# A gated delta-rule chain traced in closed stretches on VectorE, with the interleaved work tied behind them

## The chip, the core and the metric

The kernel runs on one core of one Trainium2 chip. The metric is the device time of one execution in microseconds (us), the median of several runs. TensorE (PE) multiplies matrices, VectorE (DVE) and ScalarE (ACT) work on whole tiles, GpSimd (POOL) is a slower third engine for such work, and SyncE (SP) issues the transfers. Each engine takes its instructions in the order in which they were placed, so an instruction that has to wait holds up all that stand behind it on its engine.

## The reference, cut to what matters

Two transformer-like blocks on 256 tokens of width 1024. The first is a token mixer and a feed-forward part; the second is a gated delta rule with a multi-scale pooling branch beside it, then a layer that picks among 16,384 experts. The change touches the delta rule alone:

```python
q, k = _l2norm(q), _l2norm(k)                     # x * rsqrt(sum(x*x) + 1e-6), 4 heads of 128
g = jnp.cumsum(g, axis=-1)
decay = jnp.exp(jnp.where(causal, g[..., :, None] - g[..., None, :], -jnp.inf))
a_mat = jnp.where(strict, jnp.einsum("bhnid,bhnjd->bhnij", k_beta, k) * decay, 0.0)
t_mat = lax.linalg.triangular_solve(eye + a_mat, eye, left_side=True, lower=True)
w_vals = jnp.einsum("bhnij,bhnjd->bhnid", t_mat, v_beta)
...                                               # a scan over chunks with a state per head
pooled = running_mean(p, window) - p              # windows 2, 4, 8, 16, a matrix each behind it
x = x + jnp.concatenate([o, pool_out], axis=-1) @ w_out
```

## The kernel before

All weights come from HBM in tiles of 128x1024. Each is split into a high part (`whi`, on ScalarE, line 210) and a low part (`wlo`, mostly on VectorE, line 223), and each projection of 128 output columns is 24 matmuls of 256 columns: 8 blocks of the inner size times three products of high and low parts (lines 366 to 368). Their results go to one of three PSUM buffers `pb`, and VectorE evacuates them (`ct`, `pp` or `zt`, a product with the row norm `rbs`), which frees the buffer.

`delta` runs two generators against each other with `weave`. **The chain** (`main`): four convolutions of k (`head`), cumulative sums of the gate, the decay matrix `dec` and its strict part `N`, sums of squares of k, their inverse root `yk` by a bit shift and three Newton steps (`rsqrt_steps`), Gram products of k (`gk`, line 1527), the spread of `byk` (line 455), N from all of these (lines 1533 and 1536), and then the inverse of eight unit triangular matrices of 128x128 (two halves `tb` of the sequence times four heads). The inverse first builds the 16x16 diagonal blocks `dg` (lines 611 to 615), copies them over the partitions with selection products (line 622, copied out to `rep` on line 624), inverts them in 15 steps of a product and a reduction on VectorE (lines 629 and 632), puts the blocks into `Z`, and doubles the block size in three levels (products on line 1566, masks on line 1576, sums on line 1571). Value products, state and output follow. **The fillers** (`filler`): the 16 projections for q, v, pooling (p) and gate (z) with what follows them (convolution taps on line 1298, silu on line 1287, pooling windows on GpSimd on line 1416, pooling products on line 1460), and, when the chain is done, the pooling half of the output projection.

The order is made in two steps. At each `yield` of a number the chain lets fillers of that weight be traced, so a `yield` between two steps of the chain puts filler instructions between them. A scheduler then places all instructions, with those of the chain at a higher priority. In the kernel before, the Newton steps for `yk` run on GpSimd (`eng=G`, lines 431 to 439), there is a `yield` before each of them, and one after each of the 15 steps of the block inverse.

Of the kernel before, what the change touches and what calls it, by code (L numbers as in the profile page):

```python
# [16 lines left out]
ALU = mybir.AluOpType  # L17
# [147 lines left out]
TY = [1.20, 8.92]  # L165
YL = [0.2, 0.64, 1.60, 3.20, 0.64, 0.72, 0.48, 0.80, 0.40, 1.92, 1.20, 0.16]
LEAD2 = 3000
LEAD3 = 3000
# [15 lines left out]
MAIN = ""  # L184
# [78 lines left out]

def weave(tc, main, fill, engines="", lead=None, leads=None):
    debt = 0.0
    engines = {getattr(mybir.EngineType, e) for e in engines.split(",") if e}
    with ExitStack() as stack:
        if engines:
            stack.enter_context(tc.manual_schedule(engines=engines))
        while True:  # L270
            with tc.high_priority(LEAD if lead is None else leads[0] if leads else lead):
                w = next(main, None)
            if w is None:
                break
            debt += w
            while debt > 0:
                g = next(fill, None)
                if g is None:
                    debt = 0.0
                    break  # L280
                debt -= g
# [6 lines left out]
class Builder:  # L288
# [110 lines left out]

    def rsqrt_steps(self, src, n, mult, add=None, floor=None, out=None, pace=0.2, eng=None):  # L400
        nc, sm = self.nc, self.s1
        V = nc.vector
        v, y, t = (sm.tile([P, 16], F32, name=k, tag=k)[:, 0:n] for k in ("rv", "ry", "rt"))
        y = y if out is None else out
# [18 lines left out]
        if short:  # L423
            for c in (0.75, 0.1875, 3.0 / 1024):
                for sp, vp, yp, tp in cut:
                    V.scalar_tensor_tensor(tp, yp, vp, yp, ALU.mult, ALU.mult)
                for sp, vp, yp, tp in cut:
                    V.scalar_tensor_tensor(yp, tp, -c, yp, ALU.add, ALU.mult)
            return y
        if eng:  # L430
            v = v if mult else src
            for _ in range(3):
                yield pace
                eng.tensor_tensor(t, v, y, ALU.mult)
                eng.tensor_tensor(t, t, y, ALU.mult)
                eng.tensor_scalar(t, t, -0.5, 1.5, ALU.mult, ALU.add)
                eng.tensor_tensor(y, y, t, ALU.mult)
            return y
# [159 lines left out]
    def inverse16(self, pool, N, Z, nb, rep):  # L598
        nc = self.nc
        V, A = nc.vector, nc.scalar  # L600
        n = Z.shape[1]
# [6 lines left out]
        for a in range(nb):  # L608
# [3 lines left out]
            else:  # L612
                V.scalar_tensor_tensor(d, N[:, :, 16 * a:16 * a + 16], bm[:, a:a + 1], d if a else eye,
                                       ALU.mult, ALU.add)
        V.tensor_tensor(dg, dg, dg2, ALU.add)
        A.copy(zd, eye)
# [9 lines left out]
        for j in range(1, 16):  # L626
# [4 lines left out]
            for h in hv:  # L631
                V.tensor_reduce(zd[:, h, j:j + 1], tmp[:, h, 0:j + 1], mybir.AxisListType.X, ALU.add)
            yield 0.6
        for a in range(nb):
# [604 lines left out]
    def delta(self, xs, pre, rs):  # L1239
# [5 lines left out]
        with tc.tile_pool(name="del", bufs=1) as dp:  # L1245
# [239 lines left out]
            def sums(tb):  # L1485
# [3 lines left out]
                for h in range(4):  # L1489
                    mm(ss[:, h:h + 1], sq[:, h, :], self.ones[:, 0:1], start=True, stop=True)  # L1490
                V.scalar_tensor_tensor(so[:, tb * 4:tb * 4 + 4], ss[:, 0:4], 1.0 / P, qe[:, tb * 4:tb * 4 + 4],
                                       ALU.mult, ALU.add)

            def main():
                sl = [slice(0, 4), slice(4, 8)]
# [24 lines left out]
                yield YL[1]  # L1520
                yield from self.rsqrt_steps(ss[:, 0:8], 8, 1.0, 4e-6, out=yk, pace=YL[11], eng=G)
                V.tensor_tensor(byk, beta.rearrange("p b h -> p (b h)"), yk, ALU.mult)
                gk = [b4(self.pa()), b4(self.pa())]
                for tb in range(2):
                    ts = slice(tb * P, tb * P + P)
                    for h in range(4):
                        mm(gk[tb][:, h, :], k[:, h, ts], k[:, h, ts], start=True, stop=True)
                yield YL[1]
                for tb in range(2):
# [7 lines left out]
                    G.tensor_tensor(dec[:, sl[tb], :], dec[:, sl[tb], :], tri.unsqueeze(1).to_broadcast([P, 4, P]), ALU.mult)  # L1537
                next(inv)
                yield YL[2]
                next(inv)  # L1540
                yield YL[3]
                for w in inv:
                    yield YL[4]
# [97 lines left out]

            weave(tc, main(), fl, MAIN, LEAD3)
            st["acc"] = [self.pa() for _ in range(4)]
# [371 lines left out]
```

## Time and profile before

| | |
|---|---|
| median of 3 runs | 1428.66 us (1424.08 to 1431.24) |
| the profiled execution | 1422.52 us, of which its span is 1420.7 us |
| TensorE busy | 1347.7 us (95% of the span) |
| VectorE busy | 1002.0 us (71%) |
| ScalarE busy | 683.5 us (48%) |
| GpSimd busy | 284.3 us (20%) |
| mean granted TensorE clock | 0.978 of full speed |

Busy times overlap. The span is from the first to the last instruction; the time of the execution also holds what lies around it. The granted clock has two levels, 2.4 GHz (1.00) and 1.2 GHz (0.50); a window that shows a number between them holds a change. Matmuls are pipelined, so TensorE's busy time is not TensorE at its peak.

### The profile page before, as it was taken

The page shows a single profiled execution, that of the slowest core. Times are in us where ns is not written, and L with a number is a line of the kernel's source. Part 1 is how long each engine was busy: PE and PEld are TensorE (multiplying, and loading weights), DVE is VectorE, ACT ScalarE, POOL GpSimd, SP SyncE. Part 2 cuts the span into 40 slices and gives each one's busy share as a digit, 9 for nine tenths or more (in the row PEclk, how much of TensorE's full clock was granted, in tenths as well). Part 3 has the DMA queues.
Part 4 walks back from the last instruction along what each step waited for, and adds up shares of the span by engine and source line. Part 5 has one row for each costly group of instructions (what it writes and reads, how often), then busy time and mean ns, then how long its engine had stood idle before and what let it go on. Part 6 is the DMA issues. An engine that isn't in the chain of part 4 may idle for free.

```text
span 1420.7 us, 26854 instructions
## 1 busy us (share of the span) xinstructions
PE 1347.7 (95%) x10570; PEld 1256.6 (88%) x10570; DVE 1002.0 (71%) x2060; ACT 683.5 (48%) x1242; POOL 284.3 (20%) x244
## 2 busy tenths in 40 slices
PE   7989999999999879999879999999999999999998
PEld 6888989999989868999879999999998888888886
DVE  7865768888869955899974777777875555555554
ACT  3522455565566502564534554444444555555554
POOL 5511351100034400202341000000002222222221
PEclk9899999999999989999989999999999999999999
DMA  6231434665524402444445444444446666666663
GB/s 221 65 98 47 142 127 135 208 227 180 189 92 149 134 16 75 151 163 164 153 144 179 158 155 149 149 149 143 150 154 205 193 194 193 193 193 193 193 193 118
DMA packets 64318, 217.88 MB, mean 153 GB/s; under 512 B 10272, under 2 KB 11232, under 8 KB 64064
## 3 DMA queue, kind: packets, MB, share of 16 engines
q1 hardware_dynamic: 59376, 212.76, 45.9%
q0 software_dynamic: 976, 2.71, 0.7%
q8 instruction: 83, 1.36, 0.4%
q10 hardware_dynamic: 3840, 0.70, 0.4%
q14 instruction: 43, 0.35, 0.1%
HBM read 214.69 MB, written 1.44 MB: 152 GB/s over the span
## 4 chain that ended last, share of the span: by engine, by line
PE 70%; DVE 21%; issue 3%; ACT 3%; POOL 3%; DMA 1%; SPq 0%; ACTq 0%; DVEq 0%; POOLq 0%
PE pa L1923 24%; PE pb L366 10%; PE pb L368 9%; PE pb L367 9%; DVE wlo L223 5%; PE pa L367 3%; PE pa L366 3%; PE pa L368 3%; PE pa L1566 1%; DVE x L1866 1%; DVE scr L1687 1%; DVE eg L1870 1%; PE pb L1877 1%; ACT whi L210 1%; POOL wlo L223 1%
## 5 line engine op out<-in xcount | busy, mean ns | idle before, releaser
L210 ACT ACTIVATE whi<-raw 128x1024 fp32r<-128x1024 f32 x396 | 418.4, 1058 | 538.4 <-PE pb L367 248.5
L223 DVE TENSOR_TENSOR wlo<-raw,whi 128x1024 fp32r<-128x1024 f32 x368 | 457.5, 1244 | 252.7 <-ACT whi L210 251.0
L366 PE MATMUL pb<-xnh,whi 128*128 128x256 f32 x1024 | 297.2, 291 | 13.8 <-DVE scr L1851 8.3
L368 PE MATMUL pb<-xnh,wlo 128*128 128x256 f32 x1024 | 291.0, 285 | 11.5 <-POOL wlo L223 6.9
L367 PE MATMUL pb<-xnl,whi 128*128 128x256 f32 x1024 | 290.4, 284 | 0.0
L1923 PE MATMUL pa<-whi,up 128*128 128x512 f32 x1024 | 274.7, 389 | 0.0
L1923 PEld LDWEIGHTS pa<-whi,up 128*128 128x128 f32 x1024 | 192.1, 188 | 39.8
L366 PEld LDWEIGHTS pb<-xnh,whi 128*128 128x128 f32 x1024 | 196.9, 192 | 18.2 <-PE pb L368 12.9
L368 PEld LDWEIGHTS pb<-xnh,wlo 128*128 128x128 f32 x1024 | 196.8, 192 | 13.2 <-POOL wlo L223 7.3
L367 PEld LDWEIGHTS pb<-xnl,whi 128*128 128x128 f32 x1024 | 197.2, 193 | 0.0
L366 PE MATMUL pb<-xh,whi 128*128 128x256 f32 x648 | 187.3, 289 | 0.0
L367 PE MATMUL pb<-xl,whi 128*128 128x256 f32 x648 | 184.7, 285 | 0.1
L368 PE MATMUL pb<-xh,wlo 128*128 128x256 f32 x648 | 184.7, 285 | 0.0
L1923 PE MATMUL pa<-wlo,up 128*128 128x512 f32 x512 | 158.3, 389 | 0.0
L223 POOL TENSOR_TENSOR wlo<-raw,whi 128x1024 fp32r<-128x1024 f32 x33 | 92.0, 2791 | 181.4 <-ACT whi L210 171.4
L503 POOL TENSOR_TENSOR up<-hb,up 128x256 fp32r<-128x256 f32 x32 | 45.9, 1435 | 409.3 <-ACT up L502 409.3
L366 PEld LDWEIGHTS pb<-xh,whi 128*128 128x128 f32 x648 | 124.0, 191 | 0.9 <-ACT xh L568 0.2
L367 PEld LDWEIGHTS pb<-xl,whi 128*128 128x128 f32 x648 | 123.9, 191 | 0.8 <-DVE xl L569 0.3
L368 PEld LDWEIGHTS pb<-xh,wlo 128*128 128x128 f32 x648 | 123.6, 191 | 0.4
L1923 PEld LDWEIGHTS pa<-wlo,up 128*128 128x128 f32 x512 | 96.2, 188 | 19.9
L503 POOL TENSOR_TENSOR up<-scr,up 128x256 fp32r<-128x256 f32 x32 | 47.1, 1472 | 127.0 <-ACT up L502 127.0
L367 PE MATMUL pa<-al,whi 128*128 128x256 f32 x176 | 49.1, 281 | 0.0
(534 smaller groups left out, 2220.4 us busy)
## 6 DMA issues: line engine op xcount, KB each, us to landing
raw<-down SPq DMA_DIRECT2D x128, 512.0 KB, 3.3
raw<-up SPq DMA_DIRECT2D x128, 512.0 KB, 4.3
raw<-w_in SPq DMA_DIRECT2D x46, 512.0 KB, 3.3
raw<-w_up SPq DMA_DIRECT2D x44, 512.0 KB, 3.5
raw<-w_down SPq DMA_DIRECT2D x22, 512.0 KB, 3.7
raw<-w_out SPq DMA_DIRECT2D x16, 512.0 KB, 3.3
raw<-w_query SPq DMA_DIRECT2D x16, 512.0 KB, 3.4
x<-xT SPq DMA_DIRECT2D x4, 256.0 KB, 5.6
```

Of the source, the lines that this page charges most:

```text
L210: nc.scalar.activation(hi, self.raw[self.nh], AF.Copy)
L223: e.tensor_tensor(lo[:, a:z], raw[:, a:z], hi[:, a:z], ALU.subtract)
L366: mm(ps, w[0], x[0], start=start, stop=False, **k)
L367: mm(ps, w[0], x[1], start=False, stop=False, **k)
L368: mm(ps, w[1], x[0], start=False, stop=stop, **k)
L503: (eng or self.nc.vector).tensor_tensor(lo, src, hi.bitcast(F32), ALU.subtract)
L1566: mm(out[:, h], lh[:, tb * 4 + h, :], self.halves(rh[:, tb * 4 + h, :], l, odd), start=True, stop=True)
L1687: V.max_index(idx[:, 0:8], vals[:, 0:8], src)
L1866: V.tensor_tensor(e1, iota, over(self.i1t), ALU.is_equal)
L1870: V.tensor_tensor(eg[m], eg[0], over(self.gp[m]), ALU.mult)
L1877: mm(ps[:, n, :], e1[:, q, :, r], eg[m][:, q, :, r], start=(m == 0), stop=(m == 1))
L1923: mm(acc[tb * 2 + hf], a[:, ts], b[:, hf * 512:hf * 512 + 512], start=False, stop=(e == 127 and lo == 1), skip_group_check=True)
```

## The change

Four things are done. The Newton steps for `yk` go back to VectorE, in one run without a `yield` (`self.rsqrt`); the branch `eng` is removed. The `yield` between the Gram products and N goes, so that norm, N and diagonal blocks are traced without fillers between them; the weight of the `yield` in the convolutions (`YL[0]`) goes from 0.2 to 0.45. The 15 steps of the block inverse have one `yield` behind them all in place of one behind each. And `weave` is given a list `behind`: fillers that are traced once the list holds an instruction are placed behind it on that instruction's engine (VectorE), first behind the last instruction on the diagonal blocks, later behind the last reduction of the block inverse.

```diff
-YL = [0.2, 0.64, 1.60, 3.20, 0.64, 0.72, 0.48, 0.80, 0.40, 1.92, 1.20, 0.16]
+YL = [0.45, 0.64, 1.60, 3.20, 0.64, 0.72, 0.48, 0.80, 0.40, 1.92, 1.20, 0.16]
...
             while debt > 0:
-                g = next(fill, None)
+                with tc.issue_after(behind[0]) if behind else ExitStack():
+                    g = next(fill, None)
...
-        if eng:
-            v = v if mult else src
-            for _ in range(3):
-                yield pace
-                eng.tensor_tensor(t, v, y, ALU.mult)
-                eng.tensor_tensor(t, t, y, ALU.mult)
-                eng.tensor_scalar(t, t, -0.5, 1.5, ALU.mult, ALU.add)
-                eng.tensor_tensor(y, y, t, ALU.mult)
-            return y
...
-        V.tensor_tensor(dg, dg, dg2, ALU.add)
+        self.blocks = V.tensor_tensor(dg, dg, dg2, ALU.add).ins
...
             for h in hv:
-                V.tensor_reduce(zd[:, h, j:j + 1], tmp[:, h, 0:j + 1], mybir.AxisListType.X, ALU.add)
-            yield 0.6
+                last = V.tensor_reduce(zd[:, h, j:j + 1], tmp[:, h, 0:j + 1], mybir.AxisListType.X, ALU.add)
+        self.blocks = last.ins
+        yield 0.6
...
-                yield from self.rsqrt_steps(ss[:, 0:8], 8, 1.0, 4e-6, out=yk, pace=YL[11], eng=G)
+                self.rsqrt(ss[:, 0:8], 8, 1.0, 4e-6, out=yk)
...
                         mm(gk[tb][:, h, :], k[:, h, ts], k[:, h, ts], start=True, stop=True)
-                yield YL[1]
...
                 next(inv)
+                behind.append(self.blocks)
                 yield YL[2]
                 next(inv)
                 yield YL[3]
+                next(inv)
+                behind[0] = self.blocks
                 for w in inv:
                     yield YL[4]
...
-            weave(tc, main(), fl, MAIN, LEAD3)
+            weave(tc, main(), fl, MAIN, LEAD3, behind=behind)
```

What the scheduler makes of it is seen in the order of the instructions. Outside this stage the order is the same on every engine.

TensorE before, from the last projection matmul of the fillers to the first level of the inverse (`dg,sel` are the selection products, `con_base,Z` the transposes of Z, `xh,wlo` a projection):

```order
L368 MATMUL pb<-xh,wlo 128x256
L622 MATMUL pa<-dg,sel 128x128 x16
L1555 MATMUL pa<-con_base,Z 128x128 x8
L1566 MATMUL pa<-TT,N 128x64 x8
L1585 MATMUL pa<-q,k 128x128 x7
L1566 MATMUL pa<-Z,Y 128x64 x4
```

TensorE now, from the Gram products (`pa<-k`) to the first projection behind the selection products (`pc<-ones,sq` are column sums of squares, of k and then of q):

```order
L1522 MATMUL pa<-k 128x128 x8
L1362 MATMUL pc<-ones,sq 128x1 x12
L447 MATMUL pa<-con_base,byk 128x128 x8
L614 MATMUL pa<-dg,sel 128x128 x16
L1362 MATMUL pc<-ones,sq 128x1 x2
L367 MATMUL pb<-xh,whi 128x256
```

Before, all 16 filler projections stood ahead of the selection products and none behind them; now six full ones are done by then and ten stand behind, 72 matmuls ahead of the transposes of Z and the rest among the levels.

VectorE before, at the diagonal blocks `dg` (`wlo` is a weight split; `pw`, `z` and `zt` are pooling and gate fillers):

```order
L613 SCALAR_TENSOR_TENSOR dg<-N,con_del 128x128
L611 TENSOR_SCALAR dg_5775<-N,con_del 128x128
L223 TENSOR_TENSOR wlo<-raw,whi 128x1024
L1432 SCALAR_TENSOR_TENSOR pw<-pw,pp 128x256
L613 SCALAR_TENSOR_TENSOR dg<-N,con_del,dg 128x128
L1287 SCALAR_TENSOR_TENSOR z<-th,zt 128x256
```

VectorE now, from the end of the Newton steps to the diagonal blocks:

```order
L440 SCALAR_TENSOR_TENSOR yk<-rt,yk 128x4 x2
L1541 TENSOR_TENSOR kds<-kds,yk 128x4
L1517 TENSOR_TENSOR byk<-beta,yk 128x8
L1542 TENSOR_TENSOR beg<-beg,byk 128x4
L1543 TENSOR_SCALAR beg<-beg 128x4
L1527 SCALAR_TENSOR_TENSOR N<-pa,N 128x512
L1530 SCALAR_TENSOR_TENSOR N<-pa,yk,N 128x128 x4
L1527 SCALAR_TENSOR_TENSOR N<-pa,N 128x512
L1530 SCALAR_TENSOR_TENSOR N<-pa,yk,N 128x128 x4
L605 SCALAR_TENSOR_TENSOR dg<-N,con_del 128x128
```

No filler stands between the chain's instructions there any more; the first one is behind the last instruction on the blocks.

VectorE now, from the last reduction of the block inverse to VectorE's share of the writes of Z (`ct` evacuates a projection and frees its PSUM buffer; before, the writes of Z stood right behind the reduction):

```order
L624 TENSOR_REDUCE zd<-itmp 128x4 x2
L1291 SCALAR_TENSOR_TENSOR v<-ct,params,v 128x254
L223 TENSOR_TENSOR wlo<-raw,whi 128x1024
L1287 TENSOR_TENSOR ct<-pb,rbs 128x256
L223 TENSOR_TENSOR wlo<-raw,whi 128x1024
L631 TENSOR_SCALAR Z<-zd,con_del 128x8x16 x4
```

Two weight splits, a convolution tap and an evacuation have come between the inverse and Z.

## Rows read from the trace of the kernel before

**Rows 1.** The page's chain that ended last, shares of the span by engine.

```profile
PE 70%; DVE 21%; issue 3%; ACT 3%; POOL 3%; DMA 1%; SPq 0%; ACTq 0%; DVEq 0%; POOLq 0%
```

**Rows 2.** Waits of PE, 444 to 535 us: us in total, times, longest.

```profile
PE pa L1555 <- DVE Z L638: 8.8, 1, 8.8
PE pb L1460 <- POOL rt L435: 2.9, 1, 2.9
PE pb L1460 <- DVE pw L1432: 1.9, 1, 1.9
PE pa L1619 <- DVE vn L1615: 0.8, 1, 0.8
PE pc L1490 <- ACT osq L1488: 0.3, 1, 0.3
PE pa L1566 <- DVE rep L1576: 0.3, 1, 0.3
```

**Rows 3.** Windows of 1 us: busy PE, PEld, DVE, ACT, POOL; granted clock; DMA share, GB/s.

```profile
473.00:474.00 1.00, 0.18 (x1) 0.21 (x2) 1.00 (x4) 0.00 (x0) 1.00 (x2) 0.65 0.39 45
476.00:477.00 1.00, 1.00 (x8) 1.00 (x7) 0.78 (x3) 0.50 (x2) 0.84 (x4) 0.64 0.58 131
...
500.00:501.00 1.00, 0.00 (x0) 0.00 (x0) 1.00 (x9) 0.00 (x0) 0.00 (x0) 0.80 0.00 0
514.00:515.00 1.00, 1.00 (x11) 1.00 (x9) 0.93 (x4) 0.00 (x0) 0.00 (x0) 0.87 0.00 0
```

**Rows 4.** Timeline, PE: start, us, engine, line, operation, tiles, passes, idle before.

```profile
442.39 2.03 PE L1504 MATMUL pa<-con_del,gt 128*128 128x128 f32 x16
...
454.92 1.95 PE L1527 MATMUL pa<-k 128*128 128x128 f32 x16
...
457.42 1.84 PE L1369 MATMUL pc<-ones,sq 128*128 128x1 f32 x16
...
480.02 1.03 PE L455 MATMUL pa<-con_base,byk 128*128 128x128 f32 x8
...
494.29 3.73 PE L622 MATMUL pa<-dg,sel 128*128 128x128 f32 x32
506.78 1.94 PE L1555 MATMUL pa<-con_base,Z 128*128 128x128 f32 x8 [8.76 <-DVE Z L638]
...
525.28 1.90 PE L1566 MATMUL pa<-TT,N 128*128 128x64 f32 x16
```

**Rows 5.** Timeline of ACT: the squares of k.

```profile
453.90 1.38 ACT L517 ACTIVATE sq<-k 128x256 f32<-128x256 f32 x4
```

**Rows 6.** Timeline of DVE: small pairs, a split, taps, N, blocks, first and last inverse step.

```profile
425.04 0.22 DVE L419 TENSOR_SCALAR ry<-rv 128x1 int32<-128x1 int32 x2
...
460.27 1.21 DVE L223 TENSOR_TENSOR wlo<-raw,whi 128x1024 fp32r<-128x1024 f32 x1
...
461.80 0.86 DVE L1298 SCALAR_TENSOR_TENSOR v<-ct,params,v 128x255 f32<-128x255 f32 x2
...
482.20 1.28 DVE L1533 SCALAR_TENSOR_TENSOR N<-pa,N 128x512 f32<-128x512 f32 x2
...
485.46 0.41 DVE L1407 TENSOR_TENSOR zt<-pb,rbs 128x256 f32<-128x256 f32 x1
...
486.14 0.28 DVE L611 TENSOR_SCALAR dg<-N,con_del 128x128 f32<-128x128 f32 x1
...
496.94 0.25 DVE L629 TENSOR_TENSOR itmp<-zd,rep 128x8 f32<-128x8 f32 x2
...
504.30 0.34 DVE L632 TENSOR_REDUCE zd<-itmp 128x4 f32<-128x64 f32 x2
```

**Rows 7.** Timeline of POOL and DVE: two mask products, and VectorE beside one of them.

```profile
455.67 1.35 POOL L1537 TENSOR_TENSOR dec<-dec,con_del 128x512 f32<-128x512 f32 x1
...
465.46 1.46 POOL L1590 TENSOR_TENSOR egb<-egb,q 128x512 f32<-128x512 f32 x1 [8.45 <-DVE q L1287]
...
465.71 1.32 DVE L419 TENSOR_SCALAR yk<-rv 128x4 int32<-128x4 int32 x2
```

More of the change, by code (lines that the diff above doesn't have):

```diff
@@ L261, in drive, with weave @@
             return e.value
-def weave(tc, main, fill, engines="", lead=None, leads=None):
+def weave(tc, main, fill, engines="", lead=None, leads=None, behind=None):
     debt = 0.0
@@ L398, in rsqrt, with rsqrt_steps @@
         return drive(self.rsqrt_steps(*a, **k))
-    def rsqrt_steps(self, src, n, mult, add=None, floor=None, out=None, pace=0.2, eng=None):
+    def rsqrt_steps(self, src, n, mult, add=None, floor=None, out=None, pace=0.2):
         nc, sm = self.nc, self.s1
@@ L1492, in sums @@
                                        ALU.mult, ALU.add)
+            behind = []
             def main():
```

## The prediction

> **What bounds the kernel now.** I read the page's chain first: TensorE holds 70% of it and VectorE 21% [rows 1], so a change in one stage is worth what TensorE waits or runs slowly there. The change lies between 444 and 553 us, so I then read who TensorE waits for there. From 444 to 535 it waits 8.8 us for the diagonal blocks' inverse to reach Z, 2.9 and 1.9 us before the pooling products (the first on GpSimd, which the Newton steps share with the pooling windows, the second on VectorE), and 0.8 + 0.3 + 0.3 us at hand-offs of the chain: 15.0 us [rows 2]. Next the granted clock by microsecond. It falls from 2.4 to 1.2 GHz within the first and the last of the long idles (about 473.3 and 500.6) and is back at about 476.7 and 514.25 [rows 3]. Between the return of work (473.8 and 506.8) [rows 3, 4] and the return of the clock lie 2.9 and 7.45 us at half speed, so 1.4 + 3.7 = 5.1 us are lost. **Up for grabs: 20.1 us.** The matmuls themselves are the same before and after (297 projection matmuls between the cumulative sums and the end of the inverse, and the same chain products), so the forecast is 20.1 us less what comes back.
>
> **What the change does, with prices.** By the order listing, 57 projection matmuls instead of 89 stand ahead of the Gram products `gk`, and then none until the selection products have gone out; the other 240 follow, among the inverse's steps and its three doubling levels. So the old hole is filled and a new one is cut.
>
> *New hole: the closed stretch.* The Gram products start at 444.4 + 57 x 0.12 = 451.2 (89 projections took 10.5 us, 0.12 each) and take 1.95, to about 453.1 [rows 4]. The squares of k end at 455.3 [rows 5]; what stands ahead of them on ScalarE loses two convolution starts and gains a tanh and a copy, so I leave that time. The sums follow within 0.2 us. From 455.5 VectorE has the path to itself: 12 pairs of Newton instructions at 0.2 = 2.4 (a pair of such small ones reads 0.22), 0.2 for `byk`, half of the 1.03 us spread before the first decay product can start (0.5), 3.3 for the ten instructions on N (482.20 to 485.46), nine for the diagonal blocks at 0.28 = 2.5 [rows 4, 6], and some 0.4 us of hand-offs. That is 9.3 us, to 464.8. TensorE is in order and has nothing else queued: 464.8 - 453.1 = 11.7 us, of which 24 passes of column sums at 0.115 (2.8) and the spreads (1.0) [rows 4] are work. **Lost: 7.9 us.** Above that: the mask product of `dec` on GpSimd runs at 455.67 for 1.35 us, in the same microseconds as the Newton steps now. In the trace a pair of shift instructions took 1.32 us rather than 0.22 while a like GpSimd product ran [rows 6, 7]. So the bounds are 7.9 and 9.0; I take 8.5, since only part of the product lies beside the steps.
>
> The Trainium skill (SBUF — State Buffer, Who interferes with whom) states that a VectorE instruction with two SBUF inputs and a GpSimd instruction that reads SBUF exclude each other for a whole instruction. It speaks against putting the steps there, and by it the term is 9.0 and the time 1426.6; without any holding 7.9 and 1425.5. The 1.32 us row agrees in size.
>
> *Inverse.* After the blocks, VectorE runs: two silus, three splits of weights at 1.2, three evacuations and five convolution taps at 0.4, one small evacuation of 0.1, and the 15 inverse steps, 7.7 us (496.94 to 504.64) [rows 6]: 0.8 + 3.6 + 3.2 + 0.1 + 7.7 = 15.4, up to and with the third evacuation, which frees the PSUM buffer of the first pooling projection and which the order puts behind the last reduction. TensorE has until then the selection products (3.7), 8 passes of sums (0.9) and 48 projections (5.8) = 10.4 us [rows 4]. **Lost: 5.0 us** uncontended; GpSimd's `egb` product and its two clears now lie beside VectorE here, and one held pair costs 1.1 [rows 7], so 5.0 to 6.6; I take 5.6. The selection products start after an idle longer than both that dropped the clock [rows 3], so they run at 1.2 GHz; that cost, 1.4 to 3.7 us, lies inside this term, because VectorE and not TensorE decides when the wait ends.
>
> *Clock again.* That leaves TensorE idle for about 2 to 4 us before the pooling projection; both measured falls lie in idles of 2.9 us and more [rows 2, 3]. So 0 to 3.7 us; I take 1.4, the smaller measured loss.
>
> *Levels.* With 6 projections left among them, the doubling levels' VectorE results now stand in one queue with splits, taps and pooling. There are seven hand-offs from VectorE back to TensorE (Y, the level-0 sums, the two `rep` masks, the level-1 sums, the last Z, `vn`). Nearest row below: today's three hand-off waits, 1.4 us together [rows 2]; above, each waits for one split ahead of it, 7 x 1.2 = 8.4 [rows 6]. I take 1.4, because projections stand between product and use. *Tail:* 14 instead of 9 output-projection matmuls stand in front of the second half's value product: 5 x 0.12 = 0.6 us at most. Newton leaving GpSimd, the pacing constant and the removed branch cost nothing else; the 4.8 us of pooling waits [rows 2] are already in the 20.1.
>
> **How the numbers follow.** 8.5 + 5.6 + 1.4 + 1.4 + 0.6 = 17.5 us come back out of 20.1, a gain of 2.6. The profiled execution took 1422.52 (span 1420.7), 6.1 below the median of 1428.66; I set the difference against the median: **1426**. Bounds: 7.9 + 5.0 + 0 + 0 + 0 = 12.9 (gain 7.2, 1421.5), and 9.0 + 6.6 + 3.7 + 8.4 + 0.6 = 28.3 (loss 8.2, 1436.9). A measurement here can tell about 0.5%, 7.1 us, from no change.
>
> **Rivals.** *VectorE's backlog takes the place of the wait (slower).* Place: from the evacuation for the first pooling projection to the first level's Y. VectorE has there four splits (4.8), four Z writes (1.1, taking 0.28 each), four evacuations, ten taps, a silu and two pooling pieces (about 6.6): 12.5 us [rows 6]. TensorE has two projections and 20 more of their matmuls (8.2), the pooling product and the transposes (1.3), two groups of 16 passes (1.9 each) [rows 4]: 13.3. They are nearly level, so from about 1 us of holding on VectorE each further microsecond is TensorE's, at this and each later hand-off. At 8.4 instead of 1.4 the sum is 24.5 (1433.1); with the longer clock loss and all the holding behind the stretch (6.6) too, 27.8: 1436.4. For it: VectorE's queue is full here, and the trace shows it held by GpSimd. Against: seven in a row need a split just ahead each time. Chance 0.18 for slower by over 0.5%.
>
> *The fillers cover everything after the closed stretch (faster).* No second fall of the clock, no hand-off wait, no holding: 12.9 come back, 1421.5, and a little more if the sums and spreads keep the clock up. For it: the order puts projections between every product and its use. Chance 0.17 for faster by over 0.5%. That the change doesn't do what it says is out: the order shows the stretch closed. Within 0.5%: 0.65. The range 1419.5 to 1436.5 leaves out no more than 2 in 10 and reaches into both rivals.
>
> **What would show it.** Right: a TensorE wait for VectorE's N and diagonal blocks, near 455 to 465, of 8 to 9 us less the sums; no 8.8 us wait at the Z transposes; a wait of 2 to 4 us behind the inverse at a projection; granted clock 0.5 at the selection products, 1.00 at the levels. Wrong: the clock at 1.00 through the stretch, waits of over 1 us at most level products, or the second half's value product earlier or later than 535 us by over 7.

## The result, and the profile after

The changed kernel takes **1416.55 us** (median of 8, 1415.85 to 1419.46), the kernel before 1427.13 us beside it (median of 8, 1422.34 to 1431.24): ratio 0.9932, interval 0.9914 to 0.9951. It is faster than the range of the prediction allowed. Two later comparisons with more executions gave less: 1417.74 against 1423.13 (ratio 0.9970, 0.9953 to 0.9987) and 1418.61 against 1423.26 (0.9965, 0.9945 to 0.9985). Some executions of either kernel run 5 to 10 us longer at a mean granted clock of 0.968 to 0.974 (20 of 132 of the kernel before in the later comparisons, 3 of 24 of the changed one), and by their times (1428.66 and more) they were four of the eight of before in the first comparison, and none of the changed kernel's. The profiled executions are 1422.52 and 1416.37 us, spans 1420.7 and 1414.6: 6.1 us apart.

The waits of TensorE from 444 to 535 us, after (us in total, times, longest), to be set beside [rows 2]:

```profile
PE pa L614 <- DVE dg L607: 5.5, 1, 5.5
PE pb L367 <- DVE ct L1287: 3.5, 1, 3.5
PE pc L1362 <- ACT sq L509: 1.0, 1, 1.0
PE pa L447 <- DVE byk L1517: 0.5, 1, 0.5
PE pc L1362 <- DVE yk L420: 0.4, 1, 0.4
```

That is 10.9 us where there were 15.0. All that is left lies before 482 us; the doubling levels (485 to 521 us) have no wait in the list. TensorE's timeline (start, us, line, tiles, passes, idle before) shows the two holes and what ends them, beside [rows 4]:

```profile
450.69 1.95 PE L1522 MATMUL pa<-k 128*128 128x128 f32 x16
453.64 1.95 PE L1362 MATMUL pc<-ones,sq 128*128 128x1 f32 x16 [1.00 <-ACT sq L509]
456.00 1.84 PE L1362 MATMUL pc<-ones,sq 128*128 128x1 f32 x8 [0.41 <-DVE yk L420]
458.37 1.97 PE L447 MATMUL pa<-con_base,byk 128*128 128x128 f32 x8 [0.53 <-DVE byk L1517]
465.83 5.56 PE L614 MATMUL pa<-dg,sel 128*128 128x128 f32 x32 [5.50 <-DVE dg L607]
...
481.51 0.38 PE L367 MATMUL pb<-xh,whi 128*128 128x256 f32 x1 [3.48 <-DVE ct L1287]
...
484.49 1.03 PE L1552 MATMUL pa<-con_base,Z 128*128 128x128 f32 x8
```

The Z transposes, which waited 8.76 us in before, follow their projections at once. The spreads took 1.97 us instead of 1.03 and the selection products 5.56 instead of 3.73 [rows 4], because the clock was at its lower level. Windows of 1 us (columns as in [rows 3]):

```profile
455.00:456.00 1.00, 0.59 (x6) 0.53 (x6) 0.38 (x4) 0.20 (x1) 0.64 (x1) 0.93 0.00 0
456.00:457.00 1.00, 1.00 (x5) 1.00 (x6) 1.00 (x11) 0.00 (x0) 0.00 (x0) 0.50 0.00 0
...
469.00:470.00 1.00, 1.00 (x8) 1.00 (x8) 1.00 (x7) 0.88 (x2) 0.00 (x0) 0.75 0.89 348
...
480.00:481.00 1.00, 0.00 (x0) 0.00 (x0) 1.00 (x1) 0.91 (x4) 1.00 (x2) 1.00 0.03 8
```

It falls from 2.4 to 1.2 GHz at 455.9 us, among the column sums, and is back at 469.5. In the second hole, from 478.0 to 481.5, it stays at 1.00. VectorE's timeline shows the path that both holes follow: Newton steps, blocks, the last inverse step, the evacuation.

```profile
456.23 0.23 DVE L434 TENSOR_TENSOR rt<-rv,yk 128x4 f32<-128x4 f32 x2
...
457.80 0.23 DVE L440 SCALAR_TENSOR_TENSOR yk<-rt,yk 128x4 f32<-128x4 f32 x2
...
465.39 0.29 DVE L607 TENSOR_TENSOR dg<-dg,dg 128x128 f32<-128x128 f32 x1
...
479.25 0.34 DVE L624 TENSOR_REDUCE zd<-itmp 128x4 f32<-128x64 f32 x2
...
481.03 0.42 DVE L1287 TENSOR_TENSOR ct<-pb,rbs 128x256 f32<-128x256 f32 x1
```

GpSimd's last mask product of `dec` ended at 455.64 us, so nothing held the Newton steps:

```profile
454.37 1.27 POOL L1531 TENSOR_TENSOR dec<-dec,con_del 128x512 f32<-128x512 f32 x1
471.88 1.29 POOL L1587 TENSOR_TENSOR egb<-egb,q 128x512 f32<-128x512 f32 x1 [16.24 <-DVE zd L624]
```

The second half's values (`vb`) come near the end of the stage in both kernels. VectorE's timeline has them at 534.08 us in before,

```profile
534.08 1.12 DVE L1631 SCALAR_TENSOR_TENSOR vb<-pa,beg,vb 128x128 f32<-128x128 f32 x4 [1.25 <-PE pa L1629]
```

and at 528.24 after, so that 5.8 of the 6.1 us are won by there:

```profile
528.24 1.13 DVE L1628 SCALAR_TENSOR_TENSOR vb<-pa,beg,vb 128x128 f32<-128x128 f32 x4 [0.47 <-PE pa L1626]
```

Not all of this is the stage's own, since two executions do not reach the stage at the same time. The cumulative sums of the gate are the same instruction of TensorE in every run here. They begin at 442.39 us in before [rows 4] and at 442.01 after:

```profile
442.01 2.03 PE L1499 MATMUL pa<-con_del,gt 128*128 128x128 f32 x16
```

From there to `vb` it is 91.7 us in before and 86.2 after, so 5.5 us are the stage's and 0.4 was there ahead of it. Below, a stage is compared by this stretch.

### The profile page after: what moved, and what is told of

The parts are those of the page before. It is cut to its first block, busy times and chain, and to the rows that moved or that the text cites. A ratio compares the mean times of both kernels' runs of the same rounds, so it can differ in the third digit from the quotient of the medians.

```text
span 1414.6 us, 26852 instructions
## 1 busy us (share of the span) xinstructions
PE 1344.7 (95%) x10570; PEld 1255.3 (89%) x10570; DVE 1000.5 (71%) x2078; ACT 684.4 (48%) x1242; POOL 280.3 (20%) x232
## 3 DMA queue, kind: packets, MB, share of 16 engines
q0 software_dynamic: 976, 2.71, 0.7%
## 4 chain that ended last, share of the span: by engine, by line
PE 51%; DVE 14%; issue 2%; POOL 1%; ACT 1%; ACTq 0%; DVEq 0%
PE pa L1920 24%; PE pb L367 7%; PE pb L369 7%; PE pb L368 6%; DVE wlo L223 5%; DVE x L1863 1%; PE pa L1563 1%; DVE eg L1867 1%; PE pb L1874 1%; DVE scr L1684 1%; POOL wlo L223 1%; PE pc L1874 1%; DVE scr L1685 1%; DVE scr L1687 1%; DVE scr L1683 1%
## 5 line engine op out<-in xcount | busy, mean ns | idle before, releaser
L367 PEld LDWEIGHTS pb<-xnh,whi 128*128 128x128 f32 x1024 | 197.1, 193 | 18.3 <-PE pb L369 12.9
```

Of the source, the lines that this page charges most:

```text
L367: mm(ps, w[0], x[0], start=start, stop=False, **k)
```

## The experiments

Theory: the ties bring the gain, by keeping projections for the inverse and the levels; the closed tracing makes a hole that costs what VectorE needs. Rivals: the faster norm brings it, or the gain is not the change's at all but the scatter of the executions.

**Parts of the change.** Without the ties, everything else as changed:

```diff
-            weave(tc, main(), fl, MAIN, LEAD3, behind=behind)
+            weave(tc, main(), fl, MAIN, LEAD3)
```

> The changed kernel without the ties: later fillers may again be issued ahead of the diagonal blocks and the inverse. TensorE's order is then that of the kernel before (89 projection matmuls ahead of the Gram products, all of the rest ahead of the selection products, none among the doubling levels). Theory (the ties bring the gain, by keeping projections for the inverse and the levels): the wait of about 8 us at the Z transposes and the second fall of the clock are back, the time is 1424 to 1430. Rival (the closed tracing and VectorE's Newton steps bring it): 1414 to 1419, with an earlier chain.

Measured 1426.33 us (1422.09 to 1432.32) against 1423.94: ratio 1.0021 (1.0005 to 1.0037). TensorE's waits from 444 to 545 us:

```profile
PE pa L1552 <- DVE Z L631: 8.8, 1, 8.8
PE pb L1453 <- DVE rt L437: 3.7, 1, 3.7
PE pb L1453 <- ACT th L1278: 2.8, 1, 2.8
PE pa L1616 <- DVE vn L1612: 0.8, 1, 0.8
```

Before's waits are all back, and the pooling waits are longer. The kernel before with nothing but the Newton steps on VectorE (the `eng=G` of the call taken out):

> The kernel before with one part of the change alone: the Newton steps of k's norm on VectorE, with the pauses of the tracing kept. TensorE's order is that of before. Theory (the part is worth little without the ties): the first pooling product no longer waits behind Newton steps on GpSimd (2.9 us in before), but VectorE gets 1.8 us of steps in a full stretch; 1421 to 1424 at the median, within 1.5 us of before. Rival (the part brings the gain): 1417 to 1419.

1425.93 us against 1423.21: 1.0012 (0.9990 to 1.0034). It is no gain; its waits are those of `no_ties`, 8.8, 3.7 and 2.8 us. The expected relief at the first pooling product did not come: the wait grew from 2.9 to 3.7 us and had VectorE's Newton steps at its end. The closed tracing and the faster norm are worth nothing without the ties. The ties without the closed tracing were not run, so what the closed tracing adds to them is not shown.

The first tie alone:

```diff
                 next(inv)
-                behind[0] = self.blocks
```

> The changed kernel with the first tie alone (later fillers behind the diagonal blocks, but no longer behind the inverse). By the order listing 242 projection matmuls then stand ahead of the Z transposes and 2 behind them. Theory (the second tie keeps projections for the levels): the 3.5 us wait for the evacuation goes, the pooling waits (4.8 us in before) and the hand-offs at the levels (1.4 us) come back, so 1416.5 - 3.5 + 6.2 = about 1419, and more if the clock falls in one of these waits (1423). Rival (the second tie only costs its wait): 1413.

1421.33 us against 1423.13 (0.9993, 0.9979 to 1.0008), some 3.6 above the changed kernel on the same chip. Waits of TensorE, 444 to 540 us:

```profile
PE pa L614 <- DVE dg L607: 5.5, 1, 5.5
PE pb L1453 <- DVE pw L1425: 2.8, 1, 2.8
...
PE pb L1453 <- DVE itmp L621: 1.2, 1, 1.2
...
PE pa L1615 <- DVE vn L1611: 0.8, 1, 0.8
```

The 3.5 us wait is gone, pooling waits of 4.0 and a hand-off of 0.8 us are back, and the clock falls once more at 501 to 504 us. From the cumulative sums to `vb` it is 91.4 us, nearly the 91.7 of before. So the second tie brings most of the gain (3.6 of about 5 us by the medians, 5.1 of 5.5 in the stage).

Newton steps on GpSimd, all else as changed:

```diff
-                self.rsqrt(ss[:, 0:8], 8, 1.0, 4e-6, out=yk)
+                self.rsqrt(ss[:, 0:8], 8, 1.0, 4e-6, out=yk, eng=G)
```

> The changed kernel with the Newton steps of k's norm back on GpSimd, still without a pause in the tracing. Theory (the chain to the diagonal blocks ends TensorE's wait, everything else follows it): 12 GpSimd instructions at about 0.38 us (470.19 to 471.64 in the trace of before, four of them) are 4.6 us in place of the 1.8 us that the VectorE steps took (456.23 to 458.03 in the trace of after), so the wait for the diagonal blocks grows from 5.5 to about 8.3 us and the time by 2.8 us, to 1419.4. Rival A (the gain of the change is the faster norm): all of it goes, 1427. Rival B (the wait behind the inverse takes it up): no change, 1416.5.

1420.95 us (0.9982, 0.9965 to 0.9999; the changed kernel's ratios are 0.9965 and 0.9970). By these ratios it costs about 2 us, though the intervals overlap; in the profile the stretch to `vb` is 87.8 us instead of 86.2. Of the first gain it takes neither all nor nothing. The waits on TensorE:

```profile
PE pa L623 <- DVE dg L616: 5.4, 1, 5.4
PE pb L367 <- DVE ct L1296: 3.5, 1, 3.5
PE pa L456 <- DVE byk L1526: 2.1, 1, 2.1
```

Two details of the expectation were wrong. The wait that grows is the one for the spreads (0.5 to 2.1 us), which stand between norm and blocks; and the twelve GpSimd instructions follow each other at 0.28 us, 457.42 to 460.75, not at 0.38, so they add 1.5 us and not 2.8.

The pacing constant back at 0.2:

```diff
-YL = [0.45, 0.64, 1.60, 3.20, 0.64, 0.72, 0.48, 0.80, 0.40, 1.92, 1.20, 0.16]
+YL = [0.2, 0.64, 1.60, 3.20, 0.64, 0.72, 0.48, 0.80, 0.40, 1.92, 1.20, 0.16]
```

> The changed kernel with the pacing constant at its old 0.2. By the order listing 9 projection matmuls instead of 57 stand ahead of the Gram products; the 48 others (5.8 us) go behind the chain. Theory (the chain then begins earlier, since ScalarE squares k ahead of two splits and the exponentials, 3 to 4 us): 5.8 us of work later against 3 to 4 us won, so 1.5 to 3 us more, 1418 to 1420.5. Rival A (the chain's start is all that counts): 3 us less, 1413. Rival B (TensorE's order is all that counts): 5.8 us more, 1422.

1417.73 us, 0.9954 (0.9937 to 0.9972): like the changed kernel. `vb` stands at 528.99 us, 0.75 later, though the cumulative sums begin 0.8 earlier (441.19). The hole is longer (4.9 us at the spreads, 5.5 at the blocks) but begins earlier. By the profile this part of the change is worth some 1 to 2 us; the medians can't tell it from nothing.

**Where the inverse's wait ends, and the clock in it.** 28 matmuls on zeros fill the 5.5 us hole in front of the selection products:

```diff
             ps = self.pa()
+            if not g and clk:
+                self.clock_up(ps[:, 0:T], clk)
             for k in range(per):
```

> The changed kernel with 28 more matmuls (128x256, zeros, into a tile that is overwritten) in front of the selection products, in TensorE's idle of 5.5 us, so that the clock is back when the products start. Theory (VectorE, full from 465 us on, decides when the wait behind the inverse ends): the selection products take 1.9 instead of 3.7 us, the wait behind them for the evacuation grows by as much, from 3.5 to about 5.3 us, and the time stays at 1416.5 within 1 us. Rival (TensorE's path runs through the selection products): 1.8 us less, 1414.7.

The difference of 1.8 us in that text holds, but the products' times should read 3.7 and 5.5 us. Measured: 1419.59 us, ratio 0.9967 (0.9953 to 0.9980), which is the changed kernel's ratio. TensorE's timeline:

```profile
466.31 3.84 PE L616 MATMUL pa<-dg,sel 128*128 128x128 f32 x32 [0.92 <-DVE dg L607]
...
481.72 0.58 PE L367 MATMUL pb<-xh,whi 128*128 128x256 f32 x1 [4.92 <-DVE ct L1289]
```

and its clock, in windows of 1 us:

```profile
480.00:481.00 1.00, 0.00 (x0) 0.00 (x0) 1.00 (x2) 1.00 (x4) 1.00 (x2) 0.75 0.04 8
...
487.00:488.00 1.00, 1.00 (x10) 1.00 (x9) 1.00 (x4) 0.97 (x2) 0.25 (x1) 0.84 0.91 324
```

The products run at full clock, and the projection behind them still starts at 481.7 us: VectorE, not TensorE, ends this wait. But now the clock falls in it, at 480.5, and is back at 487.3. From 481.7 on that is 5.6 us of work at half speed, so 2.8 us lost; the stretch to `vb` is 88.3 us, 2.1 more than in the changed kernel. What was filled in one idle was waited out in the next, and there the clock fell. The other way round, 20 such matmuls ahead of the 72 projections, so that the second wait is short:

> The changed kernel with 20 more matmuls (128x256, zeros, 0.11 us each) behind the selection products, ahead of the 72 projection matmuls: 2.2 us of TensorE's second wait are filled with work that computes nothing, and the wait that is left is 3.5 - 2.2 = about 1.3 us. Theory (executions in which the clock falls in that wait lose about 2 us, as in the second profile of the changed kernel, where it was at 0.50 from 480.0 to 483.8; the others lose nothing): no fall there, 1416 in nearly all executions against 1417.7 median of the changed kernel on the chip of before. Rival (extra work in front only delays: the evacuation follows TensorE): 2.2 us more, 1419.

1417.32 us (1411.42 to 1425.27), ratio 0.9952 (0.9929 to 0.9975). The wait fell to 0.4 us and the clock stayed at 1.00 in it, yet the stretch to `vb` (529.49 us) is 87.0 us, 0.8 longer than in the changed kernel. The profiled execution took 1411.77 us, for a reason far from this stage (below).

**More fillers in the first hole**, with a first tie on the spreads and the pacing constant at 0.65:

```diff
+                behind.append(last.ins)
+                yield 0.6
                 next(inv)
-                behind.append(self.blocks)
+                behind[0] = self.blocks
```

> The changed kernel with more projections ahead of the Gram products (pacing constant 0.65 instead of 0.45: 87 matmuls instead of 57 ahead of the column sums) and a first filler tied to the spreads instead of the blocks (18 matmuls between spreads and selection products). Theory (TensorE's work sets the end, so each us of idle that is filled is gained): the sums' 1.0 and 0.4 us waits go, the wait for the blocks falls from 5.5 to about 3.3 us, the clock loses 0 to 3.7 us less: 1411 to 1413. Rival (the chain, begun 2.4 us later, or VectorE's queue takes it back): 1416 to 1419, with a longer wait for the third evacuation or new ones at the levels.

1418.56 us, 0.9974 (0.9960 to 0.9988): nothing gained. Waits of TensorE, 440 to 545 us:

```profile
PE pb L367 <- DVE ct L1287: 3.8, 1, 3.8
PE pa L614 <- DVE dg L607: 2.4, 1, 2.4
PE pc L1362 <- ACT sq L509: 2.1, 1, 2.1
```

The wait for the blocks shrank as expected, but the wait for the sums, which should have gone, is 2.1 us; the clock fell in the 3.8 us wait as well, and the stretch to `vb` is 88.4 us. With the 20 matmuls added to that:

> The kernel of fill_late with the 20 extra matmuls of clock_wait. In fill_late the projections filled 4 us of the first idle, but the time stayed, because TensorE waited 3.8 us for the third evacuation and the clock fell in that wait, from 482.9 to 489.7 (5.6 us of work at half speed, 2.8 us lost). Theory: with that wait down to about 1.6 us the clock stays up and the time falls by 2.5 to 3 us, to 1413 at the fastest and 1415.5 at the median. Rival (VectorE's queue, full from 466 to 490 us, sets the end): as fill_late, 1416 at the fastest, 1418.5 at the median.

1416.78 us, 0.9945 (0.9924 to 0.9966). The same again beside the changed kernel on one chip:

> The kernel of late_clock once more. Theory (TensorE's idle of the closed stretch and of the second wait is on the path): 1413.9 to 1417 and a median 1.5 to 2.5 us below the changed kernel's. Rival (VectorE's queue from 466 us on is the path): the same median within 0.7 us.

> The changed kernel, unchanged, beside late_clock2 on one chip. Its waits in the stage and its time are known; asked is its median against that of late_clock2 under the same conditions: 1417 to 1418 here, before at 1423, so 5 to 6 us between them, against 10.6 us in the first comparison, where four of eight executions of the kernel before took 1428.7 us and more at a lower mean clock. If that theory is right, this comparison does not repeat the 10.6 us; if the change itself is worth 10 us, it does.

1418.56 us against 1418.61 for the changed kernel: the medians are the rival's. In the profiles TensorE's waits from 444 to 535 us are 7.3 us together instead of 10.8, and the stretch to `vb` is 85.9 us instead of 87.7. Of these 1.9 us, 1.5 is what a second fall of the clock costs the changed kernel in that profile (86.2 us without it, see the scatter below); the 3.5 us of waits that went leave 0.4.

**An earlier second tie**, on step 13 of the inverse:

```diff
-        self.blocks = last.ins
+            if j == 13:
+                self.blocks = last.ins
```

> The changed kernel with the second tie on the reduction of step 13 of the inverse instead of the last, step 15. The third evacuation can then go ahead of the last one and a half steps (0.6 us each, 477.15 to 479.51 in the trace of after). Theory (that evacuation ends the wait): the wait falls from 3.5 to 2.0 to 2.5 us, and with it the time by 1.0 to 1.5 us, to 1415; executions with a second fall of the clock become rarer. Rival (Z, later by the fillers' VectorE instructions ahead of the last steps, 5 us, becomes the bound): 1418 or more, with a wait at the Z transposes or at the first level.

1422.88 us, 1.0016 (0.9994 to 1.0039): the rival. The evacuation's wait fell to 2.4 us, and a new one stands at the Z transposes:

```profile
PE pa L614 <- DVE dg L607: 5.5, 1, 5.5
PE pa L1553 <- DVE Z L632: 4.8, 1, 4.8
PE pb L367 <- DVE ct L1288: 2.4, 1, 2.4
```

**The scatter.** The kernel before and the changed one, repeated:

> The kernel before, unchanged, to see where its executions differ: they scatter over 9 us (1422.3 to 1431.2), those of the changed kernel over 3.6 us. Theory: the scatter sits at the two idles of TensorE between 465 and 514 us, where the granted clock falls and comes back at a time of its own; then a slower execution shows the same waits, a longer stretch at 1.2 GHz (about twice the lost time, so 8 us for 4 us) and a mean clock lower by 0.002 to 0.003, and nothing outside 440 to 550 us differs by over 1 us. Rival: the scatter is elsewhere (transfers, the stages before 440 or after 550 us); then the mean clock is the same in fast and slow executions, and the stages outside differ. Median 1427 either way.

> The changed kernel, unchanged, on the same chip as the three runs beside it, for its scatter and its clock. Theory (a time above the fastest is time at 1.2 GHz behind the two waits): executions of over 1418 us show a mean clock below 0.977, the others 0.978 to 0.980; the slope is about -0.9 us for each 0.001, as in the kernel before (1419.4 us at 0.980, 1432.1 at 0.971). Rival: time and clock are unrelated. Median 1416.5 if the chip does not matter.

The kernel before gave 1422.39 us (1419.41 to 1432.09; ratio 0.9995, 0.9976 to 1.0014), the changed one 1417.74. The profiled execution of before took 1422.64 us and shows the waits of the first one; none of 1428 us or more was profiled, so where these lose their time stays open. Time and clock go together: over 35 executions of the kernel before on one chip -0.88 us for each 0.001 of mean clock (correlation -0.90), over 12 of the changed one -0.57 (-0.79), where the boundary of 0.977 that was expected does not hold (1417.82 us at 0.974, 1418.84 at 0.977). The mean holds more than lost time, as the last section tells. The first theory put the cause into the stage. The second profile of the changed kernel does show a second fall there (1 us windows, then TensorE's timeline):

```profile
480.00:481.00 1.00, 1.00 (x5) 1.00 (x6) 1.00 (x2) 0.42 (x1) 0.00 (x0) 0.52 0.44 147
...
483.00:484.00 1.00, 1.00 (x8) 1.00 (x8) 1.00 (x3) 0.04 (x1) 0.00 (x0) 0.77 0.85 287
```

```profile
440.42 2.03 PE L1499 MATMUL pa<-con_del,gt 128*128 128x128 f32 x16
464.25 6.45 PE L614 MATMUL pa<-dg,sel 128*128 128x128 f32 x32 [5.49 <-DVE dg L607]
479.93 0.51 PE L367 MATMUL pb<-xh,whi 128*128 128x256 f32 x1 [2.60 <-DVE ct L1287]
```

Its `vb` is at 528.16 us and its time 1416.17, as in the first, but by luck: this execution came to the stage 1.6 us earlier (440.42 against 442.01), and the stretch to `vb` is 87.7 us instead of 86.2 (87.7 again in the third profile, which has the same fall). So the second fall costs the stage 1.5 us, and the gain of the stage is 5.5 us without it and 4.0 with it. The selection products, all at 1.2 GHz here, took 0.9 us longer than in the first profile and the wait behind them was 0.9 shorter: once more VectorE ends that wait.

What separates 1411.77 from 1416.37 us lies at 720 us, in the layer of experts, where the changed kernel's first profile has this split of weights on GpSimd:

```profile
720.06 11.45 POOL L223 TENSOR_TENSOR wlo<-raw,whi 128x1024 fp32r<-128x1024 f32 x1 [5.52 <-ACT whi L210]
```

TensorE waited 6.6 us for it, and the clock was at 0.71 from 730 to 740 us. In the profile of `clock_wait` the same split was short, and TensorE's wait 1.9 us:

```profile
722.08 2.46 POOL L223 TENSOR_TENSOR wlo<-raw,whi 128x1024 fp32r<-128x1024 f32 x1 [5.55 <-ACT whi L210]
```

So this one split was taken off GpSimd, in both kernels:

```diff
-                    S.split(G if not rate and e % GSPLIT == 0 else V)
+                    S.split(G if not rate and e % GSPLIT == 0 and e != 30 else V)
```

> The changed kernel with one weight split of the feed-forward stage (the one that began on GpSimd at 720.06 us) on VectorE instead. In the profile of the changed kernel that split took 11.45 us on GpSimd beside VectorE, TensorE waited 6.6 us for it and the clock fell in that wait; in the profile of clock_wait, 4.6 us shorter, it took 2.46 us and TensorE waited 1.9 us. Theory (this one split's length is what the executions of one kernel differ by, and neither the change nor the stage at 440 to 540 us has a part in it): the wait and the fall go, 1411 to 1413 at the median, fewer executions of 1416 to 1419. Rival (the scatter comes from the clock in the stage that the change touches): the median stays within 1 us of 1417.7 to 1418.6, or rises by the split's 1.2 us on VectorE.

> The kernel before with the same one split moved to VectorE: in its profile it took 11.90 us on GpSimd and TensorE waited 6.65 us. Theory: as much is gained as in the changed kernel, 4 to 6 us, to 1417 to 1419 at the median, so that the difference between the two kernels stays 5 to 6 us and is the stage's own. Rival (the length of that split is part of what the change gains, by another phase of the engines): the difference between the two shrinks to under 3 us.

**1408.51 us** (1406.34 to 1409.26) for the changed kernel, ratio 0.9899 (0.9879 to 0.9919); 1413.83 us (1411.19 to 1414.06) for the one before, 0.9937 (0.9917 to 0.9957). TensorE's waits from 700 to 760 us, changed kernel with the split moved:

```profile
PE pb L369 <- DVE wlo L223: 1.6, 2, 1.5
PE pc L1739 <- DVE scr L1734: 0.5, 1, 0.5
```

Both medians fall by more than expected, 10.1 us for the changed kernel (1418.61 to 1408.51, on two chips; the profiled executions differ by 7.1) and 8.3 for the other (1422.10 to 1413.83, on one), and 5.3 us remain between them. In the two profiles the stretch to `vb` is 93.4 and 88.3 us, so the stage itself has 5.1 of it. That is about what the change is worth; the split has no part in it.

The long split is the rule and not the exception: it took 11.45 to 11.92 us in 15 of the 16 profiles that have it on GpSimd, executions of 1414.7 to 1426.3 us among them, and was short in that of `clock_wait` alone. So it explains why the medians fell and why the profiled execution of `clock_wait` is so short, but not the longest executions. Each kernel with the split moved scatters over only 2.9 us, but in six executions, too few to show that the longest are gone. The changed kernel with the split moved is the fastest version of this study.

## Why the prediction was wrong

The prediction was 1426, range 1419.5 to 1436.5; what came, 1416.55, is below the range. The step that failed first is the base that the difference was set against; the second is the price of the levels and of the clock. Of the 9.45 us between the two times the base has 6.1, the terms of the sum 2.3, and some 1.0 us is left, which is less than the comparisons of these kernels differ by among themselves. What was named as a sign of being right came: the wait for the blocks, the short wait at a projection behind the inverse, no wait at the Z transposes, the lower clock at the selection products and the full one at the levels. The path was right; the base and some sizes were wrong.

- **The base.** The difference was set against the median of three, 1428.66 us, although the profiled execution took 1422.52. This is the largest error, 6.1 us. The sum was made from that execution and belonged to it: 1422.5 - 2.6 = 1419.9. Two of those three executions took 1428.66 and 1431.24 us; in five later comparisons the kernel before had medians of 1422.1 to 1423.9.
- **Closed stretch, 8.5 predicted.** Waits of 5.5, 1.0, 0.5 and 0.4 are 7.4 us. Newton ran 12 pairs from 455.62 to 458.03, 2.4 us as forecast; the holding by GpSimd, of which half was taken, was zero, since the product had ended. At the lower clock eight passes of sums took 1.84 us where sixteen took as much in before, and the spreads 1.97 instead of 1.03, 1.9 us in all. Together 9.3, 0.3 above the upper bound and 1.4 above the 7.9 without holding. VectorE's path set the end, and of the slow work only the spreads lie on it: from the end of `byk` (458.31) to the first product on N it took 1.3 us, where half a spread, 0.5, was summed (0.88 of it is the wait in the line below). The ten instructions on N took 3.6 us for 3.3, and the Gram products ended at 452.6, not 453.1. That 8.5 came so near is in part luck: the 0.6 for a holding that did not come stood in for these.

```profile
459.59 0.69 DVE L1527 SCALAR_TENSOR_TENSOR N<-pa,N 128x512 f32<-128x512 f32 x1 [0.88 <-PE pa L447]
```

- **Inverse, 5.6 predicted.** From the blocks to the end of the evacuation VectorE took 15.8 us (465.68 to 481.45) where 15.4 were summed, with one held pair of 1.41 us beside `egb`. TensorE lost 3.5 us waiting and 1.8 in the slow selection products: 5.3. The mechanism and the size were right, and `clock_sel` showed that VectorE ends this wait. The step that the second wait hides the slow clock held too.
- **Clock again, 1.4 predicted.** Zero in the first profile; 1.7 us in the second, half of the 3.4 from 480.0 to 483.4 us at which TensorE worked at 1.2 GHz (the stretch to `vb` grew by 1.5); 2.8 in `clock_sel`. The bounds of 0 and 3.7 held; it differs from one execution to the next.
- **Levels, 1.4 predicted.** No wait at all. The prediction said that projections stand between product and use, and yet took before's hand-off waits as its value. `no_ties` and `one_tie`, in which hardly a projection is left there, have the 0.8 us wait back: the forecast took the price of the kind of order that the change removes.
- **Tail, 0.6 predicted.** From `vb` to the copy of `o` it is 8.5 us in before and 8.6 after; the wait that follows, for the norm of `o`, grew from 2.0 to 2.6 us. That is the 0.6, behind the value product and not in front of it.

By the measured terms 9.3 + 5.3 + 0 + 0 + 0.6 = 15.2 us come back out of 20.1, a gain of 4.9 instead of 2.6. The traces have 5.8 us where that last wait ends (552.88 in before, 547.10 after); 0.4 of it lay ahead of the stage, and 0.5 stays unaccounted for. All this is close to the 5.3 us that remain with the split moved. The other 5.3 us of the first 10.6 did not come again in the later comparisons (5.4, 4.7, and 5.3 with the split moved), so they are put down to scatter, not to the change.

Of the rivals, the second was nearest: in the first profile no second fall, no hand-off wait, and no holding in the closed stretch (one pair was held behind it). But it had 0.17, its 12.9 us of losses were 15.2, and its time, 1421.5, again stood on the base of 1428.66. VectorE's backlog did not pass to the levels: VectorE is busy without a gap from 470 to 500 us, and from 481.5 us on TensorE has projections for as long.

The Trainium skill (SBUF — State Buffer, Who interferes with whom) was weighed as a reason against the steps on VectorE. Here it did not bite in the stretch, as the two did not meet. The row of 1.32 us that the prediction set beside it is of an instruction with one input [rows 7], so it is not the case of two inputs; the pair at 471.91 us, which has two (1.41 us, beside `egb` at 471.88), is, and agrees with it. What came of it at 720 us is told below.

## What to carry to other kernels

Make the sum against the execution that was profiled, and keep the scatter of the medians as a separate question with its own cause. Compare a stage in two profiles from an instruction that stands ahead of it in both, not by times from the start of the program. When work is held back behind a chain, price three things: the hole that the chain then leaves, at the clock it will have; the next engine's queue behind it; and the waits that go because the held work is there, which is where this change gained. Filling an idle on an engine pays only as far as no other engine ends the next wait.

## What was not expected of the hardware

- **One GpSimd instruction stretched from 2.5 to 11.5 us.** A split of 128x1024 took 2.3 to 3.7 us on GpSimd elsewhere between 640 and 755 us, 11.45 in the changed kernel at 720 us, 11.90 in the kernel before at 725, and 2.46 in `clock_wait` at 722. In that place VectorE runs instructions with two SBUF inputs one behind the other, thirteen of them from 720.21 to 729.32 us in the changed kernel; the split ended 2.2 us later, and the VectorE instruction that began at 729.36 took 2.71 us, where the same shape took 0.68 at 717.21. In `clock_wait` it was VectorE that stood instead: an instruction of 0.28 us (`gp<-scr,gp`) took 2.50. The Trainium skill (SBUF — State Buffer, Who interferes with whom) has it that the port pair which the two share is an exclusive lock, and that the order of issue decides who blocks. The two lengths agree in kind. But GpSimd was kept out for a run of VectorE instructions and not for one, though its split began (720.06) before all thirteen, and there the measurement decides.
- **Whether the clock falls in a wait differed between executions.** In the wait for the third evacuation it stayed at 1.00 through 3.48 us in one profile of the changed kernel and 3.5 us in `newton_gpsimd`; it fell at the end of 2.60 us in another profile of the changed kernel (at 480.0, the wait ended at 479.93), and in 3.8 us in `fill_late` and 4.9 in `clock_sel`.
- **It fell among the column sums.** At 455.9 us, with TensorE at 0.59 busy in that microsecond and, between waits of 1.0 and 0.4 us, sums of one column as its only work since 452.6, before the long wait for the blocks began.
- **The clock that a profile shows for the start can be missing.** `tie_step13`'s profile (mean clock 0.970) has 0.50 from 10 to 20 us, where the changed kernel's (0.978) has 1.00. Yet the same matmul takes 0.41 us there in both, the changed kernel first, where it takes 0.28 at full clock:

```profile
16.46 0.41 PE L766 MATMUL pa<-xl,whi 128*128 128x256 f32 x1
16.58 0.41 PE L767 MATMUL pa<-xl,whi 128*128 128x256 f32 x1
```

So TensorE ran at 1.2 GHz in both, and the 1.00 of the one profile is no measurement. Over half of the difference between the two means comes from there (the low stretch, 7.4 to 21.1 us, is 0.005 of 1422 us at half clock), so a mean clock does not turn into lost time by itself.
